# Scan of a Mamba-2 layer: the meta tokens' state product with 128 rows, and the 64-column products of a group in one run

## The chip, the core and the metric

One core of one Trainium2 chip runs the whole layer in one launch. The metric is device time in microseconds (us). TensorE is called PE below, VectorE DVE, ScalarE ACT, GpSimd POOL, and SyncE, which issues most loads, SP.

## What is computed

One decoder layer over 528 positions: 16 learned meta tokens and 512 tokens, width 1024. Two branches (causal pooling and a Mamba-2 scan) are gated, summed and projected, and a squared-ReLU MLP follows. The change touches the scan alone. Cut to what matters, the reference is:

```python
# ssd_chunked: chunks of 128 positions; the 16 meta tokens are a leading partial chunk
xdt    = x * dt                                    # (chunk, 128, group, 4 heads, 64)
a_cs   = cumsum(dt * a)                            # within a chunk
cb     = einsum("bclgn,bcsgn->bclsg", C, B)
y_diag = einsum("bclsg,bclsgr,bcsgrp->bclgrp", cb, lmat, xdt)
decay  = exp(a_cs[:, :, -1:] - a_cs)
states = einsum("bclgn,bclgr,bclgrp->bcgrpn", B, decay, xdt)
h[c+1] = exp(a_cs[:, c, -1]) * h[c] + states[c]    # scan over chunks
y_off  = einsum("bclgn,bcgrpn,bclgr->bclgrp", C, h, exp(a_cs))
y      = y_diag + y_off
```

There are 8 groups of 4 heads, 64 channels to a head and 128 state columns to a group. The state that the meta tokens leave is the first term: `states` of their chunk.

## The kernel before

Everything is kept transposed: channels on the 128 partitions, positions along the free dimension. All weights pass through blocks of 128x1024 that are loaded by SP, rounded by ACT (`whi`) and completed by DVE (`wlo = raw - whi`), and each projection is three products of such halves (`whi` with the high and low half of the activation, `wlo` with the high half: lines 191 and 193 in `proj`). These are 128x128 stationary operands with 264 or 512 streaming columns.

The scan runs group by group. For group g, `ssd(g, cur)` is a generator, and `weave` takes one step of it and one step of the filling work in turn; the filling work is the projection of group g + 1 (`group_proj`: `px` for B, C and two blocks of x, sometimes a gate `pgp`, then `pz`). In group 4 the output projection of the first half (`out_half`, tile `pso`) is woven in as well; in the last group the filling is `out_part` (tile `psp`).

The written order is not the order on an engine: a scheduler orders the instructions of each engine by priority and by estimated times before the launch, so that po products can stand in the middle of a block's px products. `tc.issue_after(ins)` puts the instructions of its block behind `ins` on their engine. On the chip each engine then takes its instructions in that fixed order.

The steps of `ssd` are:

1. Transposes (lines 473 to 488): B of three chunks and of the 16 meta tokens into the PSUM tile `ptb`, x of the meta tokens into `ptm`, x of four chunks into two tiles `ptx`. ACT copies B out as `btok` (three chunks, 128 rows) and `btm` (16 rows); DVE multiplies x by dt into `xdt` and `xdtm`, and these by the decay into `xdd` and `xddm` (16 rows, decay `decm`). Then ACT and DVE make the decay matrix in place in `abc` (also called `dm`).
2. `pcb` = C times B for four chunks (line 522); DVE masks it into `cbm`. Then the states: line 529 multiplies `btm` (16 rows) and `xddm`, lines 530 to 532 the three chunks with 128 rows, all 256 columns wide, into two tiles `pst`. ACT copies the first state out; DVE makes the other three one after another (lines 538 and 539), and multiplies `dm` by `cbm` (line 542).
3. For each half i of the group's 256 channels: `po` = state times C for four chunks (line 550, 128 columns), `py` = `xdt` times `dm` for four chunks and two heads (line 556, 64 columns each; the two heads go to PSUM partitions 0 to 63 and 64 to 127), and then DVE makes y from both (lines 559 to 563). Each half is a step of its own, so that a step of the filling work comes between them in the written order.
4. Square, sum over the channels by PE (tile `png`), root and reciprocal, scaling, and the halves `yh`, `yl` for the output projection.

`dt_out` makes the decays once, before group 0. PSUM is two double-bank tiles (`psum2`: px, pz, pgp, pso, psp) and four single-bank tiles (`psum1`: ptb, ptm, ptx, pcb, pst, po, py, png), which are handed out in turn.

Of the kernel before, what the change touches and what calls it, by code (L numbers as in the profile page):

```python
# [9 lines left out]
F32 = mybir.dt.float32  # L10
F32R = mybir.dt.float32r
AF = mybir.ActivationFunctionType
ALU = mybir.AluOpType

P = 128
D = 1024
SEQ = 512
NM = 16
# [4 lines left out]
R = 4  # L23
HEADS = 32
# [39 lines left out]
def kernel(ctx: ExitStack, tc, xT, x, w, f1, f2, vec, fnw, out):  # L64
    nc = tc.nc
    act, dve, pe, pool = nc.scalar, nc.vector, nc.tensor, nc.gpsimd

    const = ctx.enter_context(tc.tile_pool(name="const", bufs=1, side="left"))
# [64 lines left out]
    ident = const.tile([P, P], F32, name="ident")  # L133
# [16 lines left out]
    def col(off, i, n=P):  # L150
        return vs[:n, off + i : off + i + 1]

    dtok = const.tile([P, 2, 4, HEADS], F32, name="dtok")
    dtm = const.tile([NM, 2, HEADS], F32, name="dtm")
    dec = const.tile([P, 4, HEADS], F32, name="dec")
    cdec = const.tile([P, 4, HEADS], F32, name="cdec")
    decm = const.tile([NM, HEADS], F32, name="decm")

    u_stack = ExitStack()
    up = u_stack.enter_context(tc.tile_pool(name="up", bufs=1, side="left"))  # L160
# [12 lines left out]
    def psum1(name):  # L173
        return psb.tile([P, 512], F32, tag="s", name=name)
# [40 lines left out]
    H = HEADS  # L215
# [105 lines left out]
    for t, name in ((rsh, "dgh"), (rsl, "dgl")):  # L321
        d = pre.tile([NT, 6, NT], F32R, tag="sq", name=name, bufs=2)
# [3 lines left out]
    for i in range(2):  # L326
        pb = psum1(f"pb1_{i}")
        c = slice(3 * i, 3 * i + 3)
        for n in range(2):
            pe.matmul(pb[:, : 3 * NT], ones_r[:NT], dg[n][:, c, :].rearrange("p a b -> p (a b)"),  # L330
                      start=n == 0, stop=n == 1)
# [11 lines left out]
    for c in range(4):  # L343
        r = slice(c * H, (c + 1) * H)
# [19 lines left out]
    for c in (slice(0, P), slice(P, W)):  # L364
        n = c.stop - c.start
# [4 lines left out]
    def dt_out():  # L370

        pt = psum1("pt_dt")
        for j, src in enumerate((dt, acs)):
            pe.transpose(pt[:, j * P : (j + 1) * P], src[:, :P], ident)
            pe.transpose(pt[:NM, 256 + j * H : 256 + (j + 1) * H], src[:H, P:], ident[:H, :H])
        dve.tensor_copy(dtok.rearrange("p a c h -> p (a c h)"), pt[:, :256])
        dve.tensor_copy(dtm.rearrange("p a h -> p (a h)"), pt[:NM, 256 : 256 + 2 * H])
        pq = psum1("pq_dt")
        pe.matmul(pq[:, :128], sel[:, 0, :], dtok[:, 1, :, :].rearrange("p c h -> p (c h)"),
                  start=True, stop=True)  # L380
        pe.matmul(pq[:NM, 128 : 128 + H], sel[:NM, 1, :NM], dtm[:, 1, :], start=True, stop=True)
        fl = lambda t: t.rearrange("p c h -> p (c h)")
        dve.tensor_tensor(fl(dec), pq[:, :128], fl(dtok[:, 1, :, :]), op=ALU.subtract)
        dve.tensor_tensor(decm, pq[:NM, 128 : 128 + H], dtm[:, 1, :], op=ALU.subtract)
        act.activation(fl(dec), fl(dec), AF.Exp)
        act.activation(decm, decm, AF.Exp)
        act.activation(fl(cdec), pq[:, :128], AF.Exp)


# [65 lines left out]
    def bc(ap, n):  # L455
        return ap.unsqueeze(len(ap.shape)).to_broadcast(list(ap.shape) + [n])

    def ssd(g, cur):

        xc, bt, ct, zt = cur  # L460
        hs = slice(R * g, R * g + R)
        tok = lambda c: slice(NM + c * P, NM + (c + 1) * P)
        ctok = lambda c: slice(c * P, (c + 1) * P)
        flat = lambda t: t.rearrange("p r d -> p (r d)")
# [1 line left out]
        abc_load[g] = nc.gpsimd.dma_start(abc, acs_d[hs, :].partition_broadcast(P))  # L466

        xdt = gs.tile([P, 4, R, 64], F32, tag="xdt", name=f"xdt{g}")
        xdtm = gs.tile([NM, R, 64], F32, tag="xdtm", name=f"xdtm{g}")
        btok = gs.tile([P, 3, P], F32, tag="btok", name=f"btok{g}")  # L470
        btm = gs.tile([NM, P], F32, tag="btm", name=f"btm{g}")
        ptb = psum1(f"ptb{g}")
        for c in range(3):
            pe.transpose(ptb[:, c * P : (c + 1) * P], bt[:, tok(c)], ident)
        pe.transpose(ptb[:NM, 3 * P :], bt[:, :NM], ident)
        act.copy(btok.rearrange("p c n -> p (c n)"), ptb[:, : 3 * P])
        b_meta[g] = act.copy(btm, ptb[:NM, 3 * P :])
        pm = psum1(f"ptm{g}")
        for i in range(2):
            pe.transpose(pm[:NM, i * P : (i + 1) * P], xc[:, i, :NM], ident)  # L480
        dve.tensor_tensor(xdtm, pm[:NM, :256].rearrange("p (r d) -> p r d", r=R),
                          bc(dtm[:, 0, hs], 64), op=ALU.mult)
        for b in range(2):
            pt = psum1(f"ptx{g}_{b}")
            for c in range(2):
# [4 lines left out]
                              pt.rearrange("p (c r d) -> p c r d", c=2, r=R),  # L490
                              bc(dtok[:, 0, 2 * b : 2 * b + 2, hs], 64), op=ALU.mult)
        xdd = gs.tile([P, 3, R, 64], F32, tag="xdd", name=f"xdd{g}")
        xddm = gs.tile([NM, R, 64], F32, tag="xddm", name=f"xddm{g}")
        dve.tensor_tensor(xddm, xdtm, bc(decm[:, hs], 64), op=ALU.mult)
        x_decayed[g] = dve.tensor_tensor(xdd, xdt[:, :3, :, :], bc(dec[:, :3, hs], 64), op=ALU.mult)

        eb = gs.tile([P, 2, SEQ], F32, tag="eb", name=f"eb{g}")
# [4 lines left out]
        dm = abc.rearrange("p r (c l) -> p r c l", c=4)  # L502
# [23 lines left out]
        st = [gs.tile([P, R, 64], F32, tag=f"st{c}", name=f"st{c}_{g}") for c in range(4)]  # L526
        pss = [psum1(f"pst{g}_{b}") for b in range(2)]
        pv = [pss[c // 2][:, (c % 2) * 256 : (c % 2) * 256 + 256] for c in range(4)]
        pe.matmul(pv[0], btm, flat(xddm), start=True, stop=True)
        for c in range(3):  # L530
            pe.matmul(pv[c + 1], btok[:, c, :], xdd[:, c, :, :].rearrange("p r d -> p (r d)"),
                      start=True, stop=True)
# [7 lines left out]
        for rs_ in ((slice(0, 2), slice(2, R)) if g == G - 1 else (slice(0, R),)):  # L540
            n = rs_.stop - rs_.start
            masked[g] = dve.tensor_tensor(dm[:, rs_], dm[:, rs_], cbm.unsqueeze(1).to_broadcast([P, n, 4, P]),
                                          op=ALU.mult)
        yield

        yt = gs.tile([P, 2, SEQ], F32, tag="yt", name=f"yt{g}")
        for i in range(2):
            po = psum1(f"po{g}_{i}")
            for c in range(4):
                pe.matmul(po[:, c * P : (c + 1) * P],  # L550
                          flat(st[c])[:, i * P : (i + 1) * P], ct[:, ctok(c)], start=True, stop=True)
            py = psum1(f"py{g}_{i}")
            for c in range(4):
                for j in range(2):
                    r = 2 * i + j
                    pe.matmul(py[64 * j : 64 * j + 64, c * P : (c + 1) * P],  # L556
                              xdt[:, c, r, :], dm[:, r, c, :], start=True, stop=True)
            y = yt[:, i, :]
            dve.tensor_tensor(y, po, eb[:, i, :], op=ALU.mult)
            dve.tensor_tensor(y, y, py, op=ALU.add)  # L560
            dve.scalar_tensor_tensor(y, xc[:, i, NM:], col(V_DS, 2 * g + i), y,
                                     op0=ALU.mult, op1=ALU.add)
            dve.tensor_tensor(y, y, zt[:, i, :], op=ALU.mult)
            yield
# [14 lines left out]
        for i in range(2):  # L579
            y = yt[:, i, :]  # L580
# [8 lines left out]
    done, abc_load, masked, y_first, squared, b_meta, x_decayed = {}, {}, {}, {}, {}, {}, {}  # L589
# [22 lines left out]
    for d in range(GATES_FIRST):  # L612
        gate_pool(d, True)
        if d == 0:
            dt_out()
# [3 lines left out]
    gs = gc_stack.enter_context(tc.tile_pool(name="gs", bufs=1, side="left", reuse_waits="tile"))  # L619
# [137 lines left out]
    for g in range(G):  # L757
        nxt = group_tiles(g + 1) if g + 1 < G else None
        fill = [group_proj(g + 1, nxt, GATE_AT.get(g))] if nxt else [out_part()]
        if g == 4:  # L760
            fill = [out_half()] + fill
        if g in SUMS_AT:
            fill.append(sums_of_u(SUMS_AT.index(g), g))
        if g in SETS_AT:
            fill.append(weight_sums_at(g))
        weave(ssd(g, cur), fill, 2 if g == 4 else 1)
        cur = nxt
# [633 lines left out]
    for c in range(NC - 1):  # L1401
        z, e = c == 0, c == NC - 2

        n = 2 * c + 3
# [63 lines left out]
    c = NC - 1  # L1468
# [10 lines left out]
    end = slice(768, 1024)  # L1479
# [3 lines left out]
    for t in range(4):  # L1483
        T, st = t // 2, slice((t % 2) * P, (t % 2 + 1) * P)
        n = 0
        for half in range(2):
            parts = [(0, 512)] if half == 0 or t < 3 else [(0, 256), (256, 256)]
            for a, m in parts:
# [3 lines left out]
                i = 0  # L1492
# [4 lines left out]
                for k, seg in ((1, (A11, 3)[T]), (0, (A12, A22)[T])):  # L1497
                    wh, wl = wq[k, half]
                    for p in range(2):
                        x0 = p * 512 + a  # L1500
                        f = i == 0 and not (T == 0 and half == 0) and not a
                        i += 1
                        for lhs, rhs in ((hh, wh), (hh, wl), (hl, wh)):
                            pe.matmul(ps, lhs[:, p, seg, st], rhs[:, x0 : x0 + m], start=f and lhs is hh and rhs is wh,
                                      stop=i == 4 and lhs is hl, skip_group_check=True)
# [150 lines left out]
```

## Time and profile before

| | us |
|---|---|
| median of 3 runs | 1003.0 |
| lowest and highest run | 1002.24 and 1005.76 |
| span of the profiled execution | 1001.4 |
| PE busy | 993.2 (99%) |
| DVE busy | 793.2 (79%) |
| ACT busy | 602.8 (60%) |
| POOL busy | 88.1 (9%) |
| granted TensorE clock, mean | 0.999 |

The span goes from the first to the last instruction of one profiled execution; a run's time has something around it. In a timeline, a row gives the start in us, the length in us, the engine, the line, the operation, the tile written and the tiles read, the shapes, and the number of instructions that the row merges. In a matmul row `16*128` means 16 rows and 128 columns of the stationary operand, and `16x256` is what streams. In the rows of one line or tile, the three numbers behind the count are the least, median and greatest duration in ns. PEld is the weight load. Matmuls overlap: the length of a row reaches to the modelled end of its last one, which may lie behind the start of the next row.

### The profile page before, as it was taken

What the parts mean: (1) busy time and instruction counts of PE and PEld (TensorE: products, weight loads), DVE (VectorE), ACT (ScalarE), POOL (GpSimd) and SP (SyncE); (2) the same over time, 40 slices, a digit from 0 to 9 for tenths busy, and PEclk for the clock granted to TensorE, in tenths of its full rate; (3) what the DMA queues carried; (4) which work ended last, traced back from release to release, by engine and by line L of the source; (5) the groups of instructions that cost most, each with busy time, mean ns of one, the idle gap of its engine ahead of it and who ended that gap; (6) DMA issues with size and microseconds to landing.
All of it is one profiled execution on the core that took longest, in us unless ns stands there. A gap on an engine that the chain in (4) does not pass through costs nothing.

```text
span 1001.4 us, 15539 instructions
## 1 busy us (share of the span) xinstructions
PE 993.2 (99%) x6095; PEld 878.3 (88%) x6095; DVE 793.2 (79%) x1147; ACT 602.8 (60%) x840; POOL 88.1 (9%) x148
## 2 busy tenths in 40 slices
PE   9999999999999999999999999999999999999997
PEld 7889898999889998988998888888889999999986
DVE  7988797979736687979789667876988888888885
ACT  8675958595827439483255343368666656656654
POOL 0022101111002011002201001121100000000000
PEclk9999999999999999999999999999999999999999
DMA  7378763678238635417978632879654464454432
GB/s 242 92 281 226 202 185 117 193 188 234 63 104 253 164 99 160 132 38 213 280 203 234 230 105 71 238 194 303 182 189 148 149 189 149 146 187 150 127 105 85
DMA packets 56202, 171.47 MB, mean 171 GB/s; under 512 B 6400, under 2 KB 7744, under 8 KB 55104
## 3 DMA queue, kind: packets, MB, share of 16 engines
q1 hardware_dynamic: 36576, 105.86, 32.5%
q0 software_dynamic: 18832, 63.71, 24.3%
q8 instruction: 48, 0.79, 0.3%
q10 hardware_dynamic: 720, 0.91, 0.3%
q14 instruction: 26, 0.21, 0.1%
HBM read 161.90 MB, written 48.40 MB: 210 GB/s over the span
## 4 chain that ended last, share of the span: by engine, by line
PE 98%; DMA 1%; ACT 0%; DVE 0%; issue 0%; SPq 0%; ACTq 0%
PE px L191 12%; PE px L1291 8%; PE alpha L1359 6%; PE pz L191 6%; PE px L193 6%; PE px L1294 4%; PE alpha L1362 3%; PE pgp L191 3%; PE pz L193 3%; PE pgs L191 3%; PE py L556 2%; PE pso L127 2%; PE po L550 2%; PE wo_alpha L1053 1%; PE pso L128 1%; PE pso L130 1%
## 5 line engine op out<-in xcount | busy, mean ns | idle before, releaser
L93 ACT CAST whi<-raw 128x1024 fp32r<-128x1024 f32 (+2 forms) x98 | 98.5, 1014 | 105.7 <-PE px L193 33.2
L95 DVE TENSOR_TENSOR wlo<-raw,whi 128x1024 fp32r<-128x1024 f32 (+2 forms) x98 | 114.7, 1176 | 50.9 <-ACT whi L93 33.1
L191 PE MATMUL px<-uh,whi 128*128 128x264 f32 (+1 forms) x448 | 113.2, 291 | 0.0
L193 PE MATMUL px<-ul,whi 128*128 128x264 f32 (+1 forms) x448 | 110.5, 285 | 0.0
L191 PEld LDWEIGHTS px<-uh,whi 128*128 128x128 f32 x448 | 84.6, 189 | 1.8 <-issue 1.4
L193 PEld LDWEIGHTS px<-ul,whi 128*128 128x128 f32 x448 | 84.3, 188 | 0.4 <-issue 0.2
L1066 DVE TENSOR_TENSOR ht<-ht,alpha 128x1024 f32<-128x1024 f32 x35 | 42.7, 1219 | 29.1 <-PE alpha L1359 29.1
L989 ACT CAST shi<-rawf 128x1024 fp32r<-128x1024 f32 x42 | 44.2, 1051 | 28.7 <-PE alpha L1362 18.2
L191 PE MATMUL px<-uh,wlo 128*128 128x264 f32 (+1 forms) x448 | 58.5, 283 | 0.0
L191 PEld LDWEIGHTS px<-uh,wlo 128*128 128x128 f32 x448 | 55.9, 188 | 0.0
L1359 PE MATMUL alpha<-shi,hh 128*128 128x512 f32 x140 | 55.2, 394 | 0.0
L1362 PE MATMUL alpha<-shi,hl 128*128 128x512 f32 x140 | 54.7, 391 | 0.0
L990 DVE TENSOR_TENSOR slo<-rawf,shi 128x1024 fp32r<-128x1024 f32 x42 | 51.2, 1218 | 0.6 <-ACT shi L989 0.6
L1294 PE MATMUL px<-vsl,shi 128*128 128x256 f32 x192 | 47.4, 280 | 0.0
L1291 PE MATMUL px<-vsh,shi 128*128 128x256 f32 x192 | 47.4, 281 | 0.0
L193 PE MATMUL pz<-ul,whi 128*128 128x512 f32 x112 | 43.6, 390 | 0.0
L191 PE MATMUL pz<-uh,whi 128*128 128x512 f32 x112 | 43.6, 389 | 0.0
L577 DVE RECIPROCAL rs<-rs 128x128 f32<-128x128 f32 x32 | 27.2, 909 | 13.9 <-ACT rs L575 13.8
L1359 PE MATMUL alpha<-slo,hh 128*128 128x512 f32 x140 | 37.4, 389 | 0.0
L1291 PEld LDWEIGHTS px<-vsh,shi 128*128 128x128 f32 x192 | 36.2, 188 | 0.9
L1294 PEld LDWEIGHTS px<-vsl,shi 128*128 128x128 f32 x192 | 36.1, 188 | 0.9
L1294 PE MATMUL px<-vl,shi 128*128 128x256 f32 x144 | 36.1, 283 | 0.0
(558 smaller groups left out, 2859.1 us busy)
## 6 DMA issues: line engine op xcount, KB each, us to landing
raw<-in_w SPq DMA_DIRECT2D x104, 512.0 KB, 4.4
f_t<-in_f POOLq DMA_DIRECT2D x38, 512.0 KB, 6.7
f_s<-in_f POOLq DMA_DIRECT2D x26, 512.0 KB, 8.6
b<-in_f SPq DMA_DIRECT2D x21, 512.0 KB, 4.6
rawf<-in_f SPq DMA_DIRECT2D x36, 256.0 KB, 3.2
rawf<-f_t SPq DMA_DIRECT2D x36, 256.0 KB, 3.0
abc<-acs_d POOLq DMA_DIRECT2D x8, 1024.0 KB, 7.6
f_t<-f_t POOLq DMA_DIRECT2D x12, 512.0 KB, 4.4
```

Source lines behind the costliest of these rows:

```text
L93: act.copy(hi[:, c], raw[:, c])
L95: dve.tensor_tensor(lo[:, c], raw[:, c], hi[:, c].bitcast(F32), op=ALU.subtract)
L191: pe.matmul(o, wt, rhs[0][k][:, c], start=part == 0 and k == 0, stop=part == 1 and k == NK - 1)
L193: pe.matmul(o, wt, rhs[1][k][:, c], start=False, stop=False)
L577: dve.reciprocal(rs[:, ctok(c)], rs[:, ctok(c)])
L989: splits.append((act.copy(hi, src), dve.tensor_tensor(lo, src, hi.bitcast(F32), op=ALU.subtract)))
L990: dve.tensor_tensor(lo, src, hi.bitcast(F32), op=ALU.subtract)))
L1066: added[0] = dve.tensor_tensor(o, o, src, op=op)
L1291: pe.matmul(ps, m, f[k][0], start=start and not low and k == 0, stop=stop and low == 1 and k == 3, skip_group_check=True)
L1294: pe.matmul(ps, m, f[k][1], start=False, stop=False, skip_group_check=True)
L1359: pe.matmul(ps[t], hh[:, p, seg, st], m, start=bool(first and not low and p == 0), stop=bool(last and low and p == 1), skip_group_check=True)
L1362: pe.matmul(ps[t], hl[:, p, seg, st], m, start=False, stop=False, skip_group_check=True)
```

## The change

- `decm` (16 rows) becomes `wmeta` (128 rows), set to zero at the start; its first 16 rows get the decay times dt of the meta tokens, so that `xddm` comes from one multiplication instead of two.
- The transposes of the meta tokens take the first 128 positions instead of 16: 128 columns each. `btok` gets a fourth chunk and is copied out at once; `btm` and `xdtm` are gone. `xddm` has 128 rows, zero from row 16 on.
- The first state product has 128 rows.
- In step 3 both halves' `po` come first, then both halves' `py`, held behind the last `po` by `issue_after`; all of these are now in the step of half 0. DVE's work on y stays in two steps.

```diff
-    decm = const.tile([NM, HEADS], F32, name="decm")
+    wmeta = const.tile([P, HEADS], F32, name="wmeta")
+    dve.memset(wmeta, 0.0)
...
-        dve.tensor_tensor(decm, pq[:NM, 128 : 128 + H], dtm[:, 1, :], op=ALU.subtract)
+        dve.tensor_tensor(wmeta[:NM], pq[:NM, 128 : 128 + H], dtm[:, 1, :], op=ALU.subtract)
         act.activation(fl(dec), fl(dec), AF.Exp)
-        act.activation(decm, decm, AF.Exp)
+        act.activation(wmeta[:NM], wmeta[:NM], AF.Exp)
+        dve.tensor_tensor(wmeta[:NM], wmeta[:NM], dtm[:, 0, :], op=ALU.mult)
...
-        pe.transpose(ptb[:NM, 3 * P :], bt[:, :NM], ident)
-        act.copy(btok.rearrange("p c n -> p (c n)"), ptb[:, : 3 * P])
-        b_meta[g] = act.copy(btm, ptb[:NM, 3 * P :])
+        pe.transpose(ptb[:, 3 * P :], bt[:, :P], ident)
+        b_meta[g] = act.copy(btok.rearrange("p c n -> p (c n)"), ptb)
         pm = psum1(f"ptm{g}")
         for i in range(2):
-            pe.transpose(pm[:NM, i * P : (i + 1) * P], xc[:, i, :NM], ident)
-        dve.tensor_tensor(xdtm, pm[:NM, :256].rearrange("p (r d) -> p r d", r=R),
-                          bc(dtm[:, 0, hs], 64), op=ALU.mult)
+            pe.transpose(pm[:, i * P : (i + 1) * P], xc[:, i, :P], ident)
+        dve.tensor_tensor(xddm, pm[:, :256].rearrange("p (r d) -> p r d", r=R),
+                          bc(wmeta[:, hs], 64), op=ALU.mult)
...
-        dve.tensor_tensor(xddm, xdtm, bc(decm[:, hs], 64), op=ALU.mult)
...
-        pe.matmul(pv[0], btm, flat(xddm), start=True, stop=True)
+        pe.matmul(pv[0], btok[:, 3, :], flat(xddm), start=True, stop=True)
...
+        po = [psum1(f"po{g}_{i}") for i in range(2)]
         for i in range(2):
-            po = psum1(f"po{g}_{i}")
             for c in range(4):
-                pe.matmul(po[:, c * P : (c + 1) * P],
+                end = pe.matmul(po[i][:, c * P : (c + 1) * P],
                           flat(st[c])[:, i * P : (i + 1) * P], ct[:, ctok(c)], start=True, stop=True)
-            py = psum1(f"py{g}_{i}")
+        py = [psum1(f"py{g}_{i}") for i in range(2)]
+        for i in range(2):
             for c in range(4):
                 for j in range(2):
                     r = 2 * i + j
-                    pe.matmul(py[64 * j : 64 * j + 64, c * P : (c + 1) * P],
-                              xdt[:, c, r, :], dm[:, r, c, :], start=True, stop=True)
+                    with tc.issue_after(end.ins):
+                        pe.matmul(py[i][64 * j : 64 * j + 64, c * P : (c + 1) * P],
+                                  xdt[:, c, r, :], dm[:, r, c, :], start=True, stop=True)
+        for i in range(2):
             y = yt[:, i, :]
-            dve.tensor_tensor(y, po, eb[:, i, :], op=ALU.mult)
-            dve.tensor_tensor(y, y, py, op=ALU.add)
+            dve.tensor_tensor(y, po[i], eb[:, i, :], op=ALU.mult)
+            dve.tensor_tensor(y, y, py[i], op=ALU.add)
```

More of the change, by code (lines that the diff above doesn't have):

```diff
@@ L468, in ssd @@
         xdt = gs.tile([P, 4, R, 64], F32, tag="xdt", name=f"xdt{g}")
-        xdtm = gs.tile([NM, R, 64], F32, tag="xdtm", name=f"xdtm{g}")
-        btok = gs.tile([P, 3, P], F32, tag="btok", name=f"btok{g}")
-        btm = gs.tile([NM, P], F32, tag="btm", name=f"btm{g}")
+        btok = gs.tile([P, 4, P], F32, tag="btok", name=f"btok{g}")
+        xddm = gs.tile([P, R, 64], F32, tag="xddm", name=f"xddm{g}")
         ptb = psum1(f"ptb{g}")
@@ L492, in ssd @@
         xdd = gs.tile([P, 3, R, 64], F32, tag="xdd", name=f"xdd{g}")
-        xddm = gs.tile([NM, R, 64], F32, tag="xddm", name=f"xddm{g}")
-        dve.tensor_tensor(xddm, xdtm, bc(decm[:, hs], 64), op=ALU.mult)
         x_decayed[g] = dve.tensor_tensor(xdd, xdt[:, :3, :, :], bc(dec[:, :3, hs], 64), op=ALU.mult)
```

## The prediction

> **What bounds the kernel now.** I read the page first: busy shares, then the chain of work that ended last.
>
> ```profile
> span 1001.4 us, 15539 instructions
> PE 993.2 (99%) x6095; PEld 878.3 (88%) x6095; DVE 793.2 (79%) x1147; ACT 602.8 (60%) x840; POOL 88.1 (9%) x148
> PE 98%; DMA 1%; ACT 0%; DVE 0%; issue 0%; SPq 0%; ACTq 0%
> ```
>
> TensorE is busy for 99% of the span and 98% of the chain is its own instructions: the end is set by one matmul behind the other. A busy PE can still hide a wait shorter than a matmul's modelled length, so I asked next for all that PE waited for, over the whole span:
>
> ```profile
> PE pdt L233 <- DVE ones_r L138: 1.5, 1, 1.5
> PE px L181 <- DVE xl L241: 0.6, 2, 0.3
> ```
>
> That is 2.1 us, all of it in the opening. In the scan nobody keeps PE waiting, so time is taken off only where matmuls follow each other faster, and every such nanosecond reaches the end. What counts of a matmul is then the distance from its start to the next start, not its duration. I read those distances from the timeline of PE.
>
> **The state products.** First group 1 around line 529 (an fp32 product is two records):
>
> ```profile
> 119.93 1.06 PE L522 MATMUL pcb<-ct,bt 128*128 128x128 f32 x8
> 120.92 0.69 PE L529 MATMUL pst<-xddm,btm 16*128 16x256 f32 x2
> 121.54 1.56 PE L531 MATMUL pst<-xdd,btok 128*128 128x256 f32 x6
> 122.76 0.47 PE L191 MATMUL px<-uh,whi 128*128 128x258 f32 x1
> 123.06 0.28 PE L193 MATMUL px<-ul,whi 128*128 128x258 f32 x1
> 123.18 0.28 PE L191 MATMUL px<-uh,whi 128*128 128x258 f32 x1
> ...
> 121.86 1.03 PE L531 MATMUL pst<-xdd,btok 128*128 128x256 f32 x4
> ...
> L522 PE MATMUL pcb<-ct,bt x64: 272/275/276, 76.4 to 438.8; 128*128 128x128 f32 x64
> ...
> 439.04 0.69 PE L529 MATMUL pst<-xddm,btm 16*128 16x256 f32 x2
> 439.67 0.70 PE L531 MATMUL pst<-xdd,btok 128*128 128x256 f32 x2
> ```
>
> Undisturbed distances: a 128x128 record of pcb (1.06 - 0.275)/7 = 0.112 us; the second to sixth records of L531 run from 121.86, and with one px of 123.18 - 123.06 = 0.12 they reach 123.06, so (1.20 - 0.12)/5 = 0.216 each. The stretch from 119.93 to 123.06 holds eight pcb, eight 256-column records and a px: 8 x 0.112 + 8 x 0.216 + 0.12 = 2.74 us at those distances. It took 3.13. The 0.39 us too much lie around the two 16-row records: the last pcb before them, the two themselves (0.62 us for two) and the first 128-row record after (121.54 to 121.86 = 0.32 for 0.216). It is no wait for data: group 7, with quite other work around it, spends 439.67 - 439.04 = 0.63 on its two. I read it as the price of going to 16 rows and back. With 128 rows the meta product has the form of its three neighbours and should cost 0.216 a record. That most of its rows are zeros costs nothing: the rows of a product don't show in these distances, or 16 of them would be the cheaper ones. Eight groups: **8 x 0.39 = 3.1 us**, all on the path.
>
> **The 64-column products.** Half 0 of group 1:
>
> ```profile
> 128.65 0.60 PE L550 MATMUL po<-ct,st 128*128 128x128 f32 x4
> 129.18 1.09 PE L556 MATMUL py<-abc,xdt 128*64 128x128 f32 x16
> 130.21 0.39 PE L191 MATMUL px<-uh,whi 128*128 128x264 f32 x1
> 130.43 0.29 PE L193 MATMUL px<-ul,whi 128*128 128x264 f32 x1
> ...
> 129.45 0.83 PE L556 MATMUL py<-abc,xdt 128*64 128x128 f32 x12
> ...
> L556 PE MATMUL py<-abc,xdt x256: 272/273/324, 85.4 to 452.6; 128*64 128x128 f32 x128
> ...
> 85.45 1.02 PE py L556 x16
> 451.87 1.02 PE py L556 x16
> ```
>
> The two column halves run side by side: inside a run a pair takes (0.83 - 0.27)/5 = 0.11 us. From 128.65 to 130.43 are 1.78 us; at undisturbed distances 4 x 0.112 + 8 x 0.11 + 0.12 = 1.45. So entering and leaving a run of 64-column products costs 0.33 to 0.35 us, however long it is. The chain lists 15 runs of 16 records like these two, and group 6 has its first run cut:
>
> ```profile
> 405.89 0.61 PE L550 MATMUL po<-ct,st 128*128 128x128 f32 x4
> 406.25 0.37 PE L191 MATMUL px<-uh,whi 128*128 128x264 f32 x1
> 406.55 0.65 PE L556 MATMUL py<-abc,xdt 128*64 128x128 f32 x6
> 407.13 0.49 PE L550 MATMUL po<-ct,st 128*128 128x128 f32 x2
> 407.55 0.87 PE L556 MATMUL py<-abc,xdt 128*64 128x128 f32 x10
> 408.35 0.39 PE L193 MATMUL px<-ul,whi 128*128 128x264 f32 x1
> 408.58 0.28 PE L191 MATMUL px<-uh,whi 128*128 128x264 f32 x1
> ```
>
> Here 2.69 us passed for 6 x 0.112 + 8 x 0.11 + 2 x 0.12 = 1.79: 0.90 too much, for two entries and exits and for products that lost their partner. The change puts all po of a group ahead of all its py, so one run of 32 records per group is left and no po can come between. Seven groups lose one run, 7 x 0.34 = 2.4, and group 6 its cut one, 0.9: **3.3 us**, all on the path.
>
> **The transposes.** Those of the meta tokens get 128 columns instead of 16:
>
> ```profile
> 112.65 0.27 PE L475 MATMUL ptb<-ident,bt 128*16 128x128 f32 x1
> 112.76 0.38 PE L480 MATMUL ptm<-ident,xc 128*16 128x128 f32 x2
> 112.98 0.60 PE L488 MATMUL ptx<-ident,xc 128*128 128x128 f32 x4
> ...
> L474 PEld LDWEIGHTS ptb<-ident,bt x24: 137/139/143, 68.8 to 433.8; 128*128 128x128 f32 x24
> L475 PEld LDWEIGHTS ptb<-ident,bt x8: 89/90/90, 69.2 to 433.9; 128*16 128x16 f32 x8
> ```
>
> They start 0.11 us apart, as the 128-column products do, and nothing is lost ahead of or behind them: narrow stationary data alone costs no switch, so none comes back here. The weight load grows from 90 to 139 ns. It overlaps the transpose before it; if that cover failed, 24 loads x 0.05 = 1.2 us would be lost. I take 0, since 139 ns loads already run under transposes 0.11 us apart. The Trainium skill speaks against the change at this place: "TensorE: Matmul & The Clock Gate", section LDWEIGHTS, lets the load grow with the columns alone, P/1.2, which is 13 ns for 16 and 107 for 128. An estimate from that page, all exposed, is 24 x 93 ns = 2.2 us, and the sum below would be 4.2. The trace has a smaller step, 49 ns, and shows it hidden.
>
> **Off the path.** DVE loses a multiplication per group and ACT a copy; dt_out gains one tiny multiplication and the start a memset of 32 columns:
>
> ```profile
> L494 DVE TENSOR_TENSOR xddm<-xdtm,decm x8: 401/402/405, 74.2 to 435.6; 16x256 f32<-16x256 f32 x8
> L384 DVE TENSOR_TENSOR decm<-pq_dt,dtm x1: 169/169/169, 54.2 to 54.2; 16x32 f32<-16x32 f32 x1
> ```
>
> DVE gains 8 x 0.40 us and pays about 0.17 once at 54 us, 20 us before xddm is first made; the memset is bounded by the same 0.17, and even in front of the opening's waits it could add no more. PE covers all of it: 0. No DMA is moved.
>
> The halves' four accumulators now hold all four single-bank PSUM buffers at once. The next taker is png, whose operands are computed from the last read of these four, so nobody waits for a bank that was free sooner before.
>
> **What the change makes wait.** All py stand behind the last po, and that needs the last state, the end of a chain on DVE:
>
> ```profile
> 132.31 0.41 DVE L539 TENSOR_TENSOR st<-st,pst 128x256 f32<-128x256 f32 x1
> 132.64 1.22 DVE L95 TENSOR_TENSOR wlo<-raw,whi 128x1024 fp32r<-128x1024 f32 x1
> ...
> 133.35 0.39 PE L550 MATMUL po<-ct,st 128*128 128x128 f32 x2
> ```
>
> In group 1 the run starts at 129.18; it would now start after 133.35, some 4 us later. Behind it on PE are the px of the next block, and DVE's additions of y wait for it. PE filled that time with px before (130.21 on), and the planned place of po kept 133.35 - 132.72 = 0.6 us behind the state. I expect px in that time again, and no cost.
>
> **The sum:** 3.1 + 3.3 = 6.4 us. The profiled execution's 1001.4 become 995.0. The median of the runs lies 1.6 above that span, so 1003.0 becomes **996.6 us**. About 0.5%, 5.0 us, is what a measurement of this kernel can tell from no change; the gain is a little over that. The forecast's own range is 995.0 (the lowest run before was 0.8 under the median, and small waits of group 7 may go) to 998.0 (a wait or two of 0.5 us appears).
>
> **Rivals.**
> - *The run of 32 does not hold, or its gain is eaten by short waits.* Px creep in between the halves, or waits of 0.4 us a group take their place. Only the state part is left: 1003.0 - 3.1 = 999.9. For it: group 6 shows a run that was cut. Against it: a late po cut it, and po can no longer come between. 0.15.
> - *The 0.39 us around L529 are not the price of 16 rows* but of something else in that product that stays: only the 3.3 are gained, 999.7. The constancy over groups speaks against it. 0.05.
> - *The wide transposes' loads are exposed*, 1.2 us: 997.8. By the rows, hardly: 0.03. With the figures that the Trainium skill gives in "TensorE: Matmul & The Clock Gate", section LDWEIGHTS, it would be 998.8.
> - *PE stands still for the last state (slower).* PE takes its instructions in a fixed order; if DVE does the next block's split (L95, 1.22) ahead of the last state's addition (0.41), the po at the head of the run comes 1.6 us late with nothing else to do on PE. In all eight groups that is 13 us against 6.4: 1009.6. It outweighs the gain from 6.4/8 = 0.8 us a group on, and makes the kernel slower by over 0.5% from 1.4 on. For it: only 0.6 us of margin in group 1. Against it: the same po stands in the same order now, and PE never waited for it. 0.08.
>
> **How the numbers follow.** The forecast keeps 0.69. Faster by over 0.5% (under 998.0): forecast and exposed loads, 0.72. Within 0.5%: the two half gains, 0.20. Slower: 0.08. The range, 995.0 to 1000.4, takes in the forecast, the loads and both half gains; it leaves out the stall and the edges.
>
> **What would show it.** Right: the two records of the meta state at 0.22 us each, no 0.32 behind them; eight runs of 32 py records, some 1.9 us from start to next start; PE's waits still 2.1 us; the scan, from the first transposes to the last py, shorter by 6 us. Wrong: more than eight runs of py, idle PE ahead of po or py with DVE's st as releaser, transposes more than 0.11 us apart.

## The result, and the profile after

The change made the kernel slower. After: 1010.95 us, the median of six runs (1007.33 to 1014.7). Before, six runs: 1003.18 (1002.24 to 1005.76). The ratio is 1.0073, with a 95% interval of 1.0059 to 1.0087. The forecast was 996.6.

The profiled execution of after took 1007.86 us, its span (1006.16 us in the trace) 4.7 us more than that of before (1001.43). Its page first: span, busy shares, TensorE by fortieths of the span, and the chain that ended last.

```profile
span 1006.2 us, 15499 instructions
PE 991.0 (98%) x6095; PEld 880.0 (87%) x6095; DVE 790.7 (79%) x1141; ACT 602.2 (60%) x832; POOL 87.9 (9%) x148
PE   9999999999799999999999999999999999999997
PE 84%; ACT 8%; issue 3%; DVE 2%; DMA 2%; POOL 1%; POOLq 0%; ACTq 0%; SPq 0%; DVEq 0%
```

The one 7 ahead of the end in the row of PE, slice 11 of 40 (251.6 to 276.7 us), says where to look; the chain, which was 98% PE, now has ACT, POOL and a DMA in it. All that PE waited for (us in total, times, longest):

```profile
PE pso L127 <- ACT yh L585: 2.4, 1, 2.4
PE pso L127 <- ACT acc L639: 1.8, 1, 1.8
PE pdt L234 <- DVE ones_r L138: 1.5, 1, 1.5
PE psp L127 <- DVE acc L668: 1.4, 1, 1.4
PE ptx L488 <- ACT rs L576: 1.1, 1, 1.1
PE po L548 <- DVE st L537: 0.3, 1, 0.3
PE pso L128 <- DVE yl L586: 0.2, 1, 0.2
```

That is 8.7 us for 2.1. In time, each group runs from its first transposition `ptb` to the next group's (the last one to the first `psl` of the output projection), in us:

| kernel | g0 | g1 | g2 | g3 | g4 | g5 | g6 | g7 |
|---|---|---|---|---|---|---|---|---|
| before | 43.29 | 49.05 | 48.75 | 48.79 | 87.44 | 43.32 | 44.01 | 54.37 |
| after | 43.17 | 48.37 | 48.64 | 48.08 | **94.90** | 42.60 | 43.59 | 55.10 |

Groups 1, 3 and 5, in which PE waits for nothing, are shorter by 0.68 to 0.72 (forecast: 0.39 + 0.34 = 0.73). Group 4 alone is longer by 7.46. Group 4 is where PE's work was filled up with the output projection: its first twelve products (`pso`) do without group 3's `yh`, the thirteenth needs it. PE's timeline there (start, length, the merged count, and in brackets the idle time and who ended it):

```profile
258.98 0.66 PE L488 MATMUL ptx<-ident,xc 128*128 128x128 f32 x4 [1.14 <-ACT rs L576]
...
264.79 0.50 PE L127 MATMUL pso<-yh,whi 128*128 128x512 f32 x1 [2.40 <-ACT yh L585]
265.51 0.80 PE L128 MATMUL pso<-yl,whi 128*128 128x512 f32 x1 [0.22 <-DVE yl L586]
266.11 0.63 PE L127 MATMUL pso<-yh,whi 128*128 128x512 f32 x1
...
273.44 0.50 PE L127 MATMUL pso<-yh,whi 128*128 128x512 f32 x1 [1.84 <-ACT acc L639]
```

That is 5.6 us of idle PE. In before the thirteenth `pso` starts at 263.17, behind the casts of `yh`, and PE does not wait. What made ACT late is one row of its own timeline, the root's and the casts' rows following from it:

```profile
250.61 1.28 ACT L499 ACT_TABLE_LOAD   x1 [9.34 <-DMA abc<-acs_d]
...
258.24 0.69 ACT L576 ACTIVATE rs<-png,eps 128x512 f32<-128x512 f32 x1
258.82 0.62 ACT L752 CAST th<-ua 128x520 fp32r<-128x520 f32 x1
...
264.13 1.12 ACT L585 CAST yh<-yt 128x512 fp32r<-128x512 f32 x2
```

ACT stands 9.34 us at the load of group 4's `abc`, with the root `rs` and `yh` of group 3 behind it in its fixed order. In before the same part was:

```profile
241.32 0.62 ACT L751 CAST th<-ua 128x520 fp32r<-128x520 f32 x1
...
248.29 1.06 ACT L501 ACTIVATE eb<-abc 64x1024 f32<-64x1024 f32 x1
...
261.82 1.13 ACT L584 CAST yh<-yt 128x512 fp32r<-128x512 f32 x2
```

Two things differ: `abc` was there in time, and the cast `th` of the sums of u stood ahead of `eb`, not behind `rs`. POOL's timeline joins the two. In after:

```profile
203.63 0.54 POOL L754 DMA_DIRECT2D t_d13h<-th  x1 [20.10 <-ACT th L752]
...
211.94 0.54 POOL L714 DMA_DIRECT2D f_t<-in_f  x1
...
238.90 0.80 POOL L722 DMA_DIRECT2D f_t<-in_f  x1 [3.77 <-DVE xc L408]
239.44 0.84 POOL L468 DMA_DIRECT2D abc<-acs_d  x1
```

and in before:

```profile
200.14 0.54 POOL L713 DMA_DIRECT2D f_t<-in_f  x1
...
228.51 0.82 POOL L721 DMA_DIRECT2D f_t<-in_f  x1 [3.64 <-DMA f_t<-f_t]
236.54 0.59 POOL L466 DMA_DIRECT2D abc<-acs_d  x1 [7.21 <-PE py L556]
```

POOL issues its transfers in order. In group 3 it has a chain of eight that sum weights (`f_t`, `f_s`, lines 714 to 722 after), the later ones each waiting for an earlier one, and then group 4's `abc`. Before, the chain ended early and POOL stood waiting for PE to free the buffer of `abc`. After, the store of `th` (group 2) held POOL 20.1 us, the chain began 11.8 us later, and `abc` was issued the moment the chain was through, 2.9 us later than before, and landed at 250.55 instead of 243.65. ACT came to that load sooner as well, at 241.27 instead of 247.00, when `abc` had been there for 3.4 us: 6.9 later and 5.7 sooner, less 3.4, make the 9.3 us for which ACT stands.

And why is `th` late? DVE's timeline of before, group 3, has the two halves' y (`yt`) apart and the sums of u (lines 741 to 744) done by 241.3:

```profile
233.86 0.68 DVE L563 TENSOR_TENSOR yt<-yt,zt 128x512 f32<-128x512 f32 x1
...
239.81 0.69 DVE L563 TENSOR_TENSOR yt<-yt,zt 128x512 f32<-128x512 f32 x1
...
240.87 0.43 DVE L744 TENSOR_TENSOR ub<-ub 128x260 f32<-128x260 f32 x1
```

In after both halves' products are there at once, and both y's are worked out first:

```profile
232.55 0.68 DVE L564 TENSOR_TENSOR yt<-yt,zt 128x512 f32<-128x512 f32 x1
...
235.65 0.68 DVE L564 TENSOR_TENSOR yt<-yt,zt 128x512 f32<-128x512 f32 x1
...
244.58 0.43 DVE L745 TENSOR_TENSOR ub<-ub 128x260 f32<-128x260 f32 x1
```

The sums end 3.7 us later here and 4.6 us later in group 2 (192.3 and 196.9), and `th` falls behind the next group's `eb` in ACT's order (group 2: 186.3 before, 202.7 after). So the theory: **half 1's y, ready 4 us sooner, pushed the sums of u back on DVE, their casts back on ACT, a store back on POOL, and with it the load that ACT, and at last PE, waits for.**

Last, the cost of standing still did not end with the idle time. Windows of after (length, then busy us of PE, PEld, DVE, ACT, POOL, then the granted clock, DMA share and GB/s):

```profile
264.00:266.00 2.00, 0.99 (x2) 0.68 (x3) 1.84 (x6) 1.98 (x4) 0.53 (x1) 0.86 0.83 261
266.00:268.00 2.00, 2.00 (x6) 1.52 (x6) 2.00 (x5) 1.99 (x4) 0.53 (x1) 0.50 0.02 5
268.00:270.00 2.00, 2.00 (x10) 1.64 (x9) 1.83 (x5) 1.98 (x5) 0.00 (x0) 0.79 0.43 133
```

At clock 0.50 the `pso` products that take 0.23 us from start to start took 0.42. From 266.11 to 269.67 ten of them passed in 3.56 us instead of 2.3: 1.3 us more. The Trainium skill, "TensorE: Matmul & The Clock Gate", section "What's actually happening", has the clock halved after an idle window of about 3.4 us. Here no stop was that long: 2.40 and 0.22 us with one product between them, and the clock fell at 265.4, in the second of them. In the kernel with the y part alone (below) two such stops, 2.39 and 0.23 us, left the clock at 1.00, and one of 2.88 us was followed by 0.50; what decides between them is not shown.

Five more executions of after had spans of 1005.6 to 1013.0 with mean clocks of 0.997 to 0.993, the two longest at 0.993 and 0.994; so the median lies 7.8 us above that of before and the profiled span only 4.7. The clock is a part of that: by an estimate from these figures, 0.003 of 1013 us is 3 us, of the 6.8 by which the longest exceeds the profiled one. Where in those executions the rest and the clock were lost isn't known.

### The profile page after: what moved, and what is told of

Same layout as the page of the kernel before. It is cut to its first block, busy times and chain, and to the rows that moved or that the text cites. A ratio compares the mean times of both kernels' runs of the same rounds, so it can differ in the third digit from the quotient of the medians.

```text
span 1006.2 us, 15499 instructions
## 1 busy us (share of the span) xinstructions
PE 991.0 (98%) x6095; PEld 880.0 (87%) x6095; DVE 790.7 (79%) x1141; ACT 602.2 (60%) x832; POOL 87.9 (9%) x148
## 4 chain that ended last, share of the span: by engine, by line
PE 84%; ACT 8%; issue 3%; DVE 2%; DMA 2%; POOL 1%; POOLq 0%; ACTq 0%; SPq 0%; DVEq 0%
PE px L1292 8%; PE px L192 8%; PE alpha L1360 6%; PE px L194 4%; PE px L1295 4%; PE alpha L1363 3%; PE pz L192 3%; PE pgs L192 3%; PE pgp L192 2%; PE wo_alpha L1054 1%; PE pf L128 1%; PE pf L127 1%; PE pz L194 1%; PE pf L130 1%; PE pgs L194 1%
```

## The experiments

The rival to the theory was that the gains themselves are not there, or that PE stands for the last state, which in the prediction was the slower side. Times below are medians against runs of before on the same chip, with the ratio's 95% interval.

### The two parts alone

State part alone (as the change has it, with the old loop for y):

> The state part of the change alone (wmeta, wide transposes, 128-row meta product); the po and py products as before. Queue theory (the loss comes from half 1's y reaching DVE some 6 us sooner, which puts the sums of u, their casts on ACT and so POOL's transfers later): this kernel leaves POOL's order as it was, so only the 3.1 us are gained, about 1000.0. Last-state theory (PE stands still because the py run waits for the last state): also about 1000, since the runs are the old ones. Wide-data theory (wide transposes or xddm from PSUM cost the time): slower than 1003, up to 1011.

1001.62 against 1002.86, ratio 0.9987 (0.9977 to 0.9997). It gains, but 1.2 us of the 3.1; the span is shorter by 1.8. The local term is there: around the state products PE's starts are 0.39 us closer in each of the eight groups, and the wide data costs nothing that shows. Part goes to group 4, 0.3 us longer because its run of `pcb` was cut by a `pso`. The rest I can't name. In groups 0, 2 and 6 the distances from `px` to `px` add up to some 0.1 us more (in group 2, 187 distances make 23.20 us instead of 23.11), in groups 1 and 3 those from `po` to `po` to 0.1 and 0.2, with no wait at either side.

The y part alone (`po` of both halves, then `py` of both, without the wide state product):

> The po/py part alone; the meta tokens' part of the states as before. Queue theory: the whole loss is here, and the 3.1 us of the state part are missing: 1011 to 1015, idle PE of some 5 us in group 4 behind the casts of yh, a wait of ACT of 9 us for abc before it. Last-state theory: also slower than before, but with PE idle ahead of po in most groups. Wide-data theory: 3.3 us faster than before, 999.9.

1009.17, ratio 1.0059 (1.0046 to 1.0072). So the loss comes with the y part. The time is 1.8 us under the range that was expected, and 1.8 under after though the gain of the state part is missing; why is not known (five runs, 1007.75 to 1011.18). The two longest waits of PE are those of after:

```profile
PE pso L127 <- ACT acc L641: 2.9, 1, 2.9
PE pso L127 <- ACT yh L587: 2.4, 1, 2.4
```

### The start of the chain: half 1's y held back on DVE

After, but DVE's work on half 1 is put behind the first convolution step of the block that fills the time, about where it was before. PE's products are written as after has them; the scheduler still put 196 of PE's 6095 records at another place.

```diff
+            k = dve.scalar_tensor_tensor(dst[:, o:], src[:, e + o - j : e + n - j], ...
+            conv_last[j] = k
...
-            dve.tensor_tensor(y, po[i], eb[:, i, :], op=ALU.mult)
+            with tc.issue_after(conv_last[1].ins) if i and g < G - 1 else nullcontext():
+                dve.tensor_tensor(y, po[i], eb[:, i, :], op=ALU.mult)
```

> The whole change, and half 1's first operation on DVE held behind the first convolution step of the filling's x block, about where it stood in the kernel before; PE's runs stay merged. The cast of the sums of u is back ahead of Square on ACT. Queue theory: abc of group 4 lands at about 244 us or sooner, no idle PE in group 4, 996.6 to 998.5. Last-state theory: the run of py waits as in the changed kernel, so 1006 or more. Wide-data theory: 1003 or more.

1000.57, ratio 0.997 (0.9959 to 0.9982). `abc` of group 4 was issued at 231.58 and landed at 239.6; group 4 took 87.04 us, and PE waits for nothing there. That is some 10 us less than after, for half 1's place in DVE's order and what the scheduler moved with it. It is 2 us short of what I expected, and this is most of it in the view of PE's waits:

```profile
PE po L551 <- DVE st L540: 1.4, 2, 0.8
```

That is PE waiting for the last state, twice (0.6 and 0.8 us), which the prediction put at nothing.

### The link on POOL: the eight weight sums moved out of group 3

After, with those eight transfers in group 5, and each later set further back. The orders of PE, ACT and DVE are those of after to the last instruction, late `th` included.

```diff
-SETS_AT = {0: 2, 1: 1, 3: 1, 5: 1, 6: 1}
-SETS_POOL = 3
+SETS_AT = {0: 2, 1: 1, 5: 1, 6: 1}
+SETS_POOL = 4
```

> The whole change, and the set of weight sums that stood on POOL's queue in group 3 is made later (SETS_AT without 3, SETS_POOL 4): the orders of PE, ACT and DVE are those of the changed kernel to the last instruction, only eight transfers no longer stand ahead of abc of group 4. Queue theory: abc of group 4 is issued at about 231 us instead of 239.4 and lands by 238; the three idle stretches of PE in group 4 (5.6 us) and the low clock behind them go, the gains of the change show: 1000 to 1004, a little slower than e3 because the small waits of the other groups stay. Last-state theory: no change, 1008 to 1012.

1000.74, ratio 0.9977 (0.9967 to 0.9987). From its POOL timeline, its ACT timeline, and the window of group 4's first 18 us:

```profile
231.22 0.55 POOL L468 DMA_DIRECT2D abc<-acs_d  x1 [18.98 <-PE py L556]
```

```profile
242.88 1.06 ACT L499 ACTIVATE eb<-abc 64x1024 f32<-64x1024 f32 x1
...
255.11 1.12 ACT L585 CAST yh<-yt 128x512 fp32r<-128x512 f32 x2
```

```profile
256.90:275.00 18.10, 18.10 (x93) 15.41 (x92) 14.47 (x21) 12.40 (x16) 0.53 (x1) 1.00 0.37 118
```

`abc` goes out as soon as PE frees its buffer, `yh` is 9 us earlier, PE never stops and keeps its clock, and group 4 takes 86.70: 8.20 less than after, and 0.74 less than before, as forecast. Nothing but POOL's queue was changed, and with it where the traffic of those transfers falls.

The control is the same edit on the kernel before:

> The kernel before with only the set of weight sums of group 3 made later, as in e4 (the orders of PE, ACT and DVE are those of the kernel before). Queue theory: abc of group 4 was in time already (no wait of PE behind it), so nothing changes: 1002 to 1004, and e4's gain is the removal of a stall that only the change has. If moving the set is a gain by itself (less traffic in the scan), this is faster by what e4 gained on the changed kernel, some 8 to 10 us: 993 to 995.

1003.59 against 1003.45, ratio 0.9999 (0.999 to 1.0009). The eight transfers cost nothing where `abc` waits for PE anyway; they cost only once the queue is late.

### The same link in the other direction

Before, with more of the same transfers in group 3, seven of them ahead of `abc`:

```diff
-SETS_AT = {0: 2, 1: 1, 3: 1, 5: 1, 6: 1}
-SETS_POOL = 3
+SETS_AT = {0: 2, 1: 1, 3: 2, 5: 1, 6: 1}
+SETS_POOL = 2
```

> The kernel before, none of the change, with a second set of weight sums ahead of abc of group 4 on POOL's queue (seven more transfers; the orders of PE, ACT and DVE stay). Queue theory: abc lands some 28 us later, about 270 us, ACT stands at eb until then with the root of group 3 behind it, and PE stands at the output projection of group 4 for some 20 us, with a low clock after it: 1020 to 1030. If a late abc were only a symptom, PE's time would not follow it: 1003 to 1006.

1028.93, ratio 1.0254 (1.0236 to 1.0271): the size that I expected, by another wait. `abc` was issued at 257.81, but ACT did not get as far as `eb`. The waits of all engines between 230 and 290 us:

```profile
ACT th L751 <- DMA t_d13h<-th: 27.1, 1, 27.1
...
PE png L572 <- ACT qhg L303: 24.2, 1, 24.2
```

The second `th` needs the buffer whose store stood behind the sums on POOL; `qhg` and PE's `png` stood behind that. So it shows that a late POOL queue alone, with PE, ACT and DVE ordered as before, stops PE, though not that it must be through `abc`.

### A better version: `py` first

If the first products at the y step are those that do not need the last state, its wait has cover. Both halves' `py` come first, both `po` behind them and with no `issue_after`; half 1's y is held as above.

```diff
-        po = [psum1(f"po{g}_{i}") for i in range(2)]
-        for i in range(2):
-            ... po products
         py = [psum1(f"py{g}_{i}") for i in range(2)]
         for i in range(2):
             ... py products
+        po = [psum1(f"po{g}_{i}") for i in range(2)]
+        for i in range(2):
+            ... po products
```

> The whole state part; the run of py is emitted ahead of both po and needs no last state; half 1's first operation on DVE is held as in e3. Queue theory with the last-state wait as a second, smaller loss: the waits of PE ahead of po of e3 (1.4 us) and of e4 go, group 4's py run is cut once (0.35 us lost): 998 to 1000. If the po waits have nothing to do with the run's place: 1000.6 as e3.

999.46 against 1003.45, ratio 0.9959 (0.9946 to 0.9973): better than both kernels. Its `py` run of group 1:

```profile
127.99 1.97 PE L553 MATMUL py<-abc,xdt 128*64 128x128 f32 x32
129.89 0.94 PE L558 MATMUL po<-ct,st 128*128 128x128 f32 x6
130.58 0.37 PE L192 MATMUL px<-uh,whi 128*128 128x264 f32 x1
```

The run starts at 127.99 instead of 134.61, and `po` may now be cut: this group's gain is still 0.82. Groups 0 to 3, 5 and 6 gain 0.64, 0.82, 0.56, 0.74, 0.72 and 1.14; the forecast had 0.73 for each of the first five and 1.29 for group 6. Group 4 loses 0.29, its run being cut in two, and group 7 0.98, where PE waits 0.7 for `yh` of group 6, 0.5 for `qhg` and 0.3 for `abc`. Against the kernel with half 1 held alone the medians leave it open (the intervals 0.9946 to 0.9973 and 0.9959 to 0.9982 overlap); the traces show the difference in groups 0 and 2, 0.5 and 0.8 us.

The same with the eight transfers moved:

> e8 with the weight sums of group 3 moved as in e4. If e8 still has a late abc in group 4, this is faster than e8 by PE's idle time there; if not, the same within 1 us: 998 to 1000.

999.5, ratio 0.9961 (0.9946 to 0.9976). No different: with half 1 held, `abc` is in time (237.6 without the move, 234.5 with it).

## Why the prediction was wrong

**What held.** Every distance that the sum was built on. Group 1 of after:

```profile
119.03 1.06 PE L520 MATMUL pcb<-ct,bt 128*128 128x128 f32 x8
119.92 0.60 PE L527 MATMUL pst<-xddm,btok 128*128 128x256 f32 x2
120.36 1.46 PE L529 MATMUL pst<-xdd,btok 128*128 128x256 f32 x6
121.47 0.47 PE L192 MATMUL px<-uh,whi 128*128 128x258 f32 x1
121.78 0.28 PE L194 MATMUL px<-ul,whi 128*128 128x258 f32 x1
...
134.61 1.97 PE L556 MATMUL py<-abc,xdt 128*64 128x128 f32 x32
136.51 0.87 PE L192 MATMUL px<-uh,wlo 128*128 128x264 f32 x5
```

The meta records are 0.22 apart, and from the first of them to the second `px` it is 121.78 - 119.03 = 2.75 us for a stretch that took 3.13: 0.38. There are eight runs of 32 `py`, 136.51 - 134.61 = 1.90 each, as listed ahead. The transposes are still 0.11 us apart with loads of 139 to 143 ns, so the longer loads cost nothing here. In the groups without a wait the gain is the forecast's.

**The step that failed** is "Off the path": "No DMA is moved", and with it, from "What the change makes wait", "I expect px in that time again, and no cost". PE's px did fill the time. But I followed the new order only on PE, and asked of DVE only whether its sum of work grew. DVE's y of half 1 moved, and with it three queues; no DMA was added, and one came 7 us later. POOL's timeline of before had the warning:

```profile
187.16 0.53 POOL L753 DMA_DIRECT2D t_d13h<-th  x1 [25.05 <-ACT th L751]
```

POOL stood 25 us for `th` of group 2 already; its chain then took from 200.14 to 228.51. POOL then stood 7.2 us until the buffer of `abc` came free; and `abc` landed at 243.65, 3.4 us before ACT turned to it. A later `th` had about that much room, some 10.6 us by these rows; in after `th` of group 2 came 16.5 us later, and the chain began 11.8 us later.

**The bill,** after against before, from the table: group 4 +7.46, group 7 +0.73, the six others -2.76, the opening -0.71, behind the scan 0.0: +4.7. (The start of the scan lies between 68.3 and 69.3 us in all these traces, so the opening is no gain of the change.) Against its forecast of -0.73, group 4 lost 8.2 us. Of these 5.6 are idle PE and about 1.3 the clock; the last 1.3 was not taken apart. A part of it is overlap lost at the four stops: a `pso` is 0.39 us long and the next starts 0.23 us after it, so by an estimate from these rows 0.16 a stop, 0.6 in all. With group 4 put right (eight sums moved) its 0.74 came, and what was then short of 6.4 lies in groups 0, 2 and 6 (0.6, 0.7 and 0.9) and 7 (1.5). Group 7's is the wait of `psp` for DVE's `acc`, 1.4 us. Group 2 has a wait of 0.35 for the last state, and `py` first brought groups 0, 2 and 6 most of theirs; so the margin of 0.6 us in group 1, which I took for all, was not there in each.

**The rivals.** The one on the slower side was PE standing for the last state at 13 us. It exists at 0.3 to 0.8 us a wait, too little to turn the sign. What turned it was on no list, so all of the chance on slower stood on the wrong mechanism. The run did hold, against the first rival: eight runs here, and nine with `py` first, where nothing forces it; but in groups 0, 2 and 6 something did eat the gain, 0.6 to 0.9 us, as that rival's other half has it.

**Open:** the distances that grew in the kernel with the state part alone, and the time and clock of after's longer executions. The best version's gain is 4.0 us of 6.4. By its trace groups 4 and 7 fall short by 1.0 and 1.7, a loss each where 0.73 was forecast; a version that mends those was not run.

## What to carry to other kernels

The price of a switch between shapes on PE can be read from start-to-start distances, and in this kernel came in to within 0.06 us in the three groups of after in which nothing waits: 0.39 us for a 16-row pair, 0.34 for a run of 64-column products. With the first alone 0.39 came at its place in every group, but only 0.13 to 0.37 of it in the groups' length (group 4 lost), so here the sum was an upper bound. But a result that is ready earlier takes a place earlier in every in-order queue behind it: follow its consumers on DVE, ACT and POOL to the next transfer whose landing holds somebody, above all where a queue stands waiting already, and hold the early result back where it is not needed. And where the order of two kinds of products is free, the ones without the newest operand went better first here.

## What was not expected of the hardware

- The clock fell to 0.50 with stops of 2.40 and 0.22 us, and was back at 268.8, some 4 us after the first product behind the longer one (264.79). In the kernel with more sums in group 3 PE stood 24.2 us, went on at 272.1, and its 512-column products were 0.43 us apart until 277.6 and 0.23 from then on. A window there:

```profile
274.00:280.00 6.00, 6.00 (x20) 4.72 (x20) 2.08 (x6) 5.91 (x7) 0.53 (x1) 0.68 0.42 135
```

- The load of `abc` took 11.1 us to land behind the last `f_t` (239.44 to 250.55), and 7.1 where POOL had stood idle before it (236.54 to 243.65). All eight loads of `abc` in after took between 4.6 and 11.1 us; with `py` first the one behind the last `f_t` took 11.2 (226.41 to 237.61).
